# Planned waits of a recurrence in TensorE's order: five numbers of a table and one new entry

## The chip, the cores and the metric

The kernel runs on one core of one Trainium2 chip. The metric is the device time of one execution in microseconds; lower is better. Three executions took 3245.59 to 3251.01 us, with a median of 3248.01 us. PE, DVE, ACT, POOL and SP are TensorE, VectorE, ScalarE, GpSimd and SyncE; PEld is TensorE's loading of weights.

## What is computed

One layer over 2048 tokens of width 1024, in float32. Its heart is a delta rule with one 64x64 state per head, beside a pooling mixer and two gates; an MLP with squared ReLU and a gated embedding follow.

```python
def rwkv7_step(S, inp):
    r, w, k, v, kk, a = inp
    sa = jnp.einsum('bhvk,bhk->bhv', S, -kk)
    S = (S * w[:, :, None, :]
         + sa[..., None] * (kk * a)[:, :, None, :]
         + v[..., None] * k[:, :, None, :])
    y = jnp.einsum('bhvk,bhk->bhv', S, r)
    return S, y
...
    for i in range(DEPTH):
        h = rmsnorm(x, g_mix[i])
        z = h @ w_in[i]
        z_rwkv = token_shift(z[..., :RWKV_COLS], mu_shift[i])
        z_pool = z[..., RWKV_COLS:RWKV_COLS + POOL_WIDTH]
        gates = jax.nn.sigmoid(z[..., RWKV_COLS + POOL_WIDTH:] + b_gates[i])
        y_a = rwkv7_mix(z_rwkv, ...) @ w_out_a[i]
        y_b = multiscale_pool_mix(z_pool, pool_w[i], pool_scale[i]) @ w_out_b[i]
        merged = gates[:, :, 0] * y_a + gates[:, :, 1] * y_b
        x = x + merged @ w_o[i]
        h = rmsnorm(x, g_mlp[i])
        x = x + jnp.square(jax.nn.relu(h @ w_ff1[i])) @ w_ff2[i]
        h = rmsnorm(x, g_ple[i])
        x = x + jax.nn.sigmoid(h @ w_ple_gate[i]) * (p[i] @ w_ple_proj[i])
    return rmsnorm(x, g_final)
```

## The kernel before

**Two kinds of work in the first part.** The tokens lie in four blocks of 512. *Dense work* is `stage_A` of blocks 0 to 3 (the projections with `w_in`, the pooling mixer, the gates and `w_out_b`), then `stage_B` of blocks 0 to 3 (`w_out_a`, the merge, `w_o`). Each float32 product is three fp32r matmuls of 128x512 into banks named `d`; `big` holds the block's normed input (in stage B the merged branches), `yx` other operands (in stage B the recurrence's output for the block), `wf` the weights. The *recurrence* goes in 32 steps of 64 tokens, all heads at once, in banks named `rp` and `rc`.

**A step of the recurrence.** Its preparation (`prep_a`, `prep`) ends on TensorE in products with `bdb`, products with `bdk`, transposes of `bdv` and transposes of `BK`. Out of the products with `bdb` comes a matrix whose 32x32 blocks `invert` inverts: they go through memory on SP's queue (`aD`, `At`), 16 pairs of operations on VectorE make the inverse (L872 and L875, tiles `Xtmp` and `Xt`), and SP's queue brings it back as `xd` (`xD`, L876 and L840). Then `chain` runs, five groups of small matmuls, each of which reads what another engine made of the one before:

- TL: products of the state `SV`; ScalarE copies them to `Tn` (L890).
- first product: `xd` times `Tn`; ScalarE copies it to `U` and `VU`.
- aof: `aof` times `U`; VectorE subtracts it from `Tn` (L914).
- second product: `xd` times the new `Tn`; VectorE and ScalarE copy it to `VU` (L921, L923).
- NB: the new state `SVn`, made by VectorE; then the outputs by RD and Ct.

`gnorm` normalises the outputs; its transposes of `ybd` are TensorE's last work of a step, after which ScalarE, POOL and SP bring the result to `yaD` in memory (L968). `load_ya` reads a block of it back into `yx` (L389 to L391).

**What sets the order.** TensorE's order is written by a planner while the kernel is built (`drive`): a clock advances with each matmul, by 0.107 us or more. At a `yield LAT[...]` a step's generator hands in how long its next group has to wait by this clock. A group whose time has come goes next, the recurrence first; otherwise a piece of dense work is taken, three matmuls as a rule. The numbers of `LAT` are planned waits and make nothing wait on the chip: there TensorE works its list in order, and each matmul waits for its operands. The other engines' and the DMA queue's orders come from a scheduler that places the rest around TensorE's order. `C0` stands between the products with `bdk` and the transposes of `bdv`, `hop` after TL, `hu` after the first product and after aof, `hv` after the second product, `hs` after the outputs. A recurrence starts `inv` (47.1) after its products with `bdb` at the earliest, and when the one before has ended; the products with `bdk` wait until the recurrence two steps back has ended; `pace` and `pace2` set the distance of the steps.

**The rest.** From about 1605 us on the last block of stage B, the MLP (seven products in place of eight) and the embedding follow.

Of the kernel before, what the change touches and what calls it, by code (L numbers as in the profile page):

```python
# [36 lines left out]
C0 = math.exp(-0.5)  # L37
# [2 lines left out]
FS, WR = 2, 4  # L40
WS, WS2, WS3, WSB = 384, 384, 512, 512

LAT = dict(p0=11.7, p0b=15.8, A=17.7, B0=2.1, B1=5.6, C0=2.0, C1=4.9, C=8.8,
           hop=3.1, hu=2.8, hv=5.3, hs=3.0, inv=47.1, gn=17.8, pace=34.4, pace2=31.5)
TC_KW = dict(schedule_with_timeline_sim=True)

W1 = NP * UT
# [51 lines left out]
def hybrid_kernel(ctx, tc, consts, x, p, g_mix, w_in, mu_shift, w0, w_decay_up, a0, w_aaa_up,  # L99
# [28 lines left out]
    def mm(out_, lhsT, rhs, start, stop, **kw):  # L128
        n = 1
        for d in rhs.shape[1:]:  # L130
            n *= d
        clock[0] += max(0.107, n * (4 if rhs.dtype == F32 else 1) / 2370.0)
        PE.matmul(out_, lhsT, rhs, start=start, stop=stop, **kw)  # L133
# [62 lines left out]
    hs = chs.enter_context(tc.tile_pool(name="hs", bufs=1, side="left"))  # L196
# [4 lines left out]
    with ExitStack() as c1:  # L201
# [438 lines left out]
        def rps():  # L640
            return psum.tile([P, 512], F32, name="rp", tag="rp", bufs=2)

        def cps():
            return psum.tile([P, 512], F32, name="rc", tag="rc", bufs=2)

        aD = [dram.tile([4 * PC, SUB, SUB], F32, name=f"aD{i}") for i in range(2)]
        xD = [dram.tile([4 * PC, SUB, SUB], F32, name=f"xD{i}") for i in range(2)]
        HOP = LAT["hop"]

        def v3(t, w=UT):  # L650
            return t.rearrange("p (n t) -> p n t", t=w)

        def pq(t):

            return t.rearrange("p (q t) -> p q t", t=L)

        def wt(name, bufs=1, w=W1):
            return rw.tile([P, w], F32, name=name, bufs=bufs)
# [3 lines left out]
        def other(hp):  # L662
            return hps[1] if hp.start == 0 else hps[0]
# [77 lines left out]
        def prep(i):  # L741
# [34 lines left out]
            for hp in hps:  # L776
                ACT.copy(out=bdv[hp, :, other(hp)], in_=v_[hp])
            passed[0], passed[1] = i, max(clock[0] + LAT["B0"], began[0] + LAT["pace" if i < NU * 3 // 4 else "pace2"])
            yield LAT["B1"]

# [7 lines left out]
            for h in range(2):  # L788
                for d in range(2):
# [3 lines left out]
                                 in_=Ast[rows, :, d * SUB:(d + 1) * SUB])  # L793
            chain_ready[i] = clock[0] + LAT["inv"]
            yield None
# [8 lines left out]
            for hp in hps:  # L804
                DVE.tensor_tensor(by_pair(TL[hp, :, other(hp)]), by_pair(pv[hp, :, 0:L]), mbc(m_k, hp), ALU.mult)
                DVE.tensor_tensor(RD[hp, :, other(hp)], pv[hp, :, L:P], minc[hp].broadcast_to([L, PC, L]), ALU.mult)
            yield LAT["C0"]
            ps = rps()
# [8 lines left out]
            for h in range(2):  # L817
                for b in range(2):
                    lo, to = h * L + b * SUB, (1 - b) * SUB
                    POOL.tensor_copy(aof[lo:lo + SUB, :, h * L + to:h * L + to + SUB],  # L820
                                     Ast[lo:lo + SUB, b::2, to:to + SUB])
            yield LAT["C1"]
            NB = rw.tile([P, PC, P], F32, name="NB", bufs=2)
# [54 lines left out]
        def chain(i):  # L878

            c_ = carried[i]  # L880
            dl, xd, aof, Ct, NB, TL, RD, SV, VU = (c_[n] for n in ("dl", "xd", "aof", "Ct", "NB", "TL", "RD", "SV", "VU"))
            SVn = bd["SV"][(i + 1) % 2]
            Y = rw.tile([P, PC, L], F32, name="Y", bufs=2)
            c_["Y"] = Y
            qs = [(q, slice(q * L, (q + 1) * L), slice(q * P, (q + 1) * P)) for q in range(PC)]

            def diag(out_, ps):

                for hp in hps:
                    ACT.copy(out=out_(hp), in_=v3(ps, P)[hp, :, hp])  # L890
            ps = cps()
            for q, sl, wl in qs:
                mm(ps[:, wl], TL[:, q, :], SV[:, q, :], True, True)
            Tn = wt("Tn")
            diag(lambda hp: pq(Tn)[hp], ps)
            yield HOP
            q2s = [slice(a * P, (a + 1) * P) for a in range(PC // 2)]

            def quarters(src, inv):

                for n, (lo, b) in enumerate((h * L + b * SUB, b) for h in range(2) for b in range(2)):
                    yield n, VU[lo:lo + SUB, b ^ inv::2, lo // L * L:(lo // L + 1) * L], pq(src)[lo:lo + SUB, b ^ inv::2, :]
            ps = cps()
            for a, sl in enumerate(q2s):
                mm(ps[:, sl], xd[:, 2 * a, :], Tn[:, sl], True, True)
            Ua = wt("U")
            ACT.copy(out=Ua, in_=ps[:, 0:W1])
            for _, to, fr in quarters(ps[:, 0:W1], 0):
                ACT.copy(out=to, in_=fr)
            yield LAT["hu"]  # L910
            ps = cps()
            for a, sl in enumerate(q2s):
                mm(ps[:, sl], aof[:, a, :], Ua[:, sl], True, True)
            DVE.tensor_tensor(Tn, Tn, ps[:, 0:W1], ALU.subtract)  # L914
            yield LAT["hu"]
            ps = cps()
            for a, sl in enumerate(q2s):
                mm(ps[:, sl], xd[:, 2 * a + 1, :], Tn[:, sl], True, True)
            for n, to, fr in quarters(ps[:, 0:W1], 1):
                if n % 2:  # L920
                    DVE.tensor_copy(to, fr)  # L921
                else:
                    ACT.copy(out=to, in_=fr)  # L923
            yield LAT["hv"]
            ps = cps()
            for q, sl, wl in qs:
                mm(ps[:, wl], NB[:, q, :], VU[:, q, :], True, True)
            for hp in hps:
                DVE.tensor_tensor(SVn[hp, :, hp], v3(ps, P)[hp, :, hp], SV[hp, :, hp], ALU.add)
            for hp in hps:  # L930
                DVE.tensor_tensor(SVn[hp, :, hp], SVn[hp, :, hp], dl[hp].unsqueeze(2).broadcast_to([L, PC, L]), ALU.mult)
            py = cps()
            for q, sl, wl in qs:
                mm(py[:, wl], RD[:, q, :], SV[:, q, :], True, False)
                mm(py[:, wl], Ct[:, q, :], VU[:, q, :], False, True)
            diag(lambda hp: Y[hp], py)
            yield LAT["hs"]
# [43 lines left out]
        p0 = {}  # L981
# [4 lines left out]
        def admit():  # L986
            kinds = [k for k, *_ in active]
            i = counts["p0"]
            if i < NU and i == counts["a"] and i not in p0 and z_done[i // NG * UT // TB]:
                with tc.high_priority():  # L990
                    p0[i] = prep0(i)
                p0_ready[i] = clock[0] + (LAT["p0b"] if i % (NG * TB // UT) == 0 else LAT["p0"])
                counts["p0"] += 1
            i = counts["a"]
            if i in p0 and passed[0] >= i - 1 and max(p0_ready[i], passed[1]) <= clock[0]:
                with tc.high_priority():
                    pa[i] = prep_a(i)
                began[0] = clock[0]
                pa_ready[i] = clock[0] + LAT["A"]
                counts["a"] += 1  # L1000
            i = counts["prep"]
            if "prep" not in kinds and i in pa and i < counts["gn_done"] + 3:
                active.append(["prep", i, prep(i), pa_ready[i], None])
                counts["prep"] += 1
            i = counts["chain"]
            if "chain" not in kinds and i < counts["prep_done"] and i < counts["gn_done"] + 2:
                active.append(["chain", i, chain(i), chain_ready[i], None])
                counts["chain"] += 1
# [640 lines left out]
```

## Time and profile before

| | |
|---|---|
| median of three executions | 3248.01 us |
| profiled execution, its own time | 3247.18 us |
| its span, first to last instruction | 3245.4 us |
| TensorE busy | 3042.8 us (94%), mean granted clock 0.974 |
| VectorE busy | 2482.3 us (76%) |
| ScalarE, GpSimd busy | 1391.9 us (43%), 1228.0 us (38%) |

Rows of the profile name a line of the code (L133 and L137 are the helpers through which all matmuls and transposes go), the engine, the operation, and out<-in by the names of the tiles; buffer numbers are left out there and kept in the order below. A number in brackets, or behind the bar after the mean, is idle time of the engine just before, with what ended it. A group's time counts overlapping instructions once.

### The profile page before, as it was taken

The page shows a single profiled execution, that of the slowest core. Times are in us where ns is not written, and L with a number is a line of the kernel's source. Part 1 is how long each engine was busy: PE and PEld are TensorE (multiplying, and loading weights), DVE is VectorE, ACT ScalarE, POOL GpSimd, SP SyncE. Part 2 cuts the span into 40 slices and gives each one's busy share as a digit, 9 for nine tenths or more (in the row PEclk, how much of TensorE's full clock was granted, in tenths as well). Part 3 has the DMA queues.
Part 4 walks back from the last instruction along what each step waited for, and adds up shares of the span by engine and source line. Part 5 has one row for each costly group of instructions (what it writes and reads, how often), then busy time and mean ns, then how long its engine had stood idle before and what let it go on. Part 6 is the DMA issues. An engine that isn't in the chain of part 4 may idle for free. (4 is left out here: it accounts for less than half of the span.)

```text
span 3245.4 us, 43606 instructions
## 1 busy us (share of the span) xinstructions
PE 3042.8 (94%) x14409; PEld 2485.6 (77%) x14409; DVE 2482.3 (76%) x5419; ACT 1391.9 (43%) x2697; POOL 1228.0 (38%) x1325
## 2 busy tenths in 40 slices
PE   7999999899999998879989999999989999998998
PEld 6777777778777876758768788788768888886787
DVE  4479888788878888985478787866568898888665
ACT  4446654455445544533144444433243334333332
POOL 4555454345333534531125456555422232222100
PEclk9999999999999999989999999999989999999999
DMA  7776767666666666767865556544554465435331
GB/s 238 246 224 211 238 205 239 231 213 206 217 212 203 206 194 221 254 218 254 281 227 165 180 193 225 193 154 153 189 188 155 143 208 207 143 129 187 119 108 69
DMA packets 422702, 636.37 MB, mean 196 GB/s; under 512 B 173710, under 2 KB 285900, under 8 KB 391244
## 3 DMA queue, kind: packets, MB, share of 16 engines
q1 hardware_dynamic: 422476, 633.58, 59.1%
q8 instruction: 114, 1.87, 0.2%
q14 instruction: 112, 0.92, 0.1%
HBM read 439.49 MB, written 193.99 MB: 195 GB/s over the span
## 5 line engine op out<-in xcount | busy, mean ns | idle before, releaser
L133 PE MATMUL d<-big,wf 128*128 128x512 f32 (+1 forms) x3288 | 851.1, 407 | 21.2 <-DVE wf L244 8.0
L133 PEld LDWEIGHTS d<-big,wf 128*128 128x128 f32 x3288 | 609.8, 193 | 159.8 <-DVE wf L244 10.5
L133 PE MATMUL d<-op 128*128 128x512 f32 x1344 | 318.4, 396 | 19.1 <-ACT op L1111 15.0
L1112 POOL TENSOR_TENSOR op<-hr,op 128x1024 fp32r<-128x1024 f32 x56 | 153.1, 2734 | 459.4 <-ACT op L1111 459.4
L133 PEld LDWEIGHTS d<-op 128*128 128x128 f32 x1344 | 254.3, 189 | 78.2 <-ACT op L1111 15.4
L1111 ACT CAST op<-hr 128x1024 fp32r<-128x1024 f32 x112 | 117.7, 1051 | 355.9 <-issue 149.6
L1112 DVE TENSOR_TENSOR op<-w,op 128x1024 fp32r<-128x1024 f32 x112 | 181.3, 1620 | 108.0 <-ACT op L1111 108.0
L872 DVE TENSOR_TENSOR Xtmp<-Xt,At 128x16 f32<-128x16 f32 (+15 forms) x512 | 241.3, 471 | 9.3
L1112 POOL TENSOR_TENSOR op<-wr,op 128x512 fp32r<-128x512 f32 x96 | 144.7, 1508 | 244.7 <-ACT op L1111 241.5
L133 PE MATMUL d<-wf,big 128*128 128x512 f32 x768 | 200.8, 415 | 20.0 <-DVE t2k L611 17.8
L133 PE MATMUL d<-yx,wf 128*128 128x512 f32 x768 | 204.3, 412 | 15.9 <-ACT yx L390 7.3
L1293 POOL TENSOR_TENSOR t<-t,t 128x512 f32<-128x512 f32 x128 | 192.7, 1515 | 68.9 <-DVE t L1303 27.5
L133 PE MATMUL d<-wg,op 128*128 128x512 f32 x768 | 184.9, 396 | 12.8 <-ACT wg L1111 6.6
L133 PEld LDWEIGHTS d<-wf,big 128*128 128x128 f32 x768 | 146.8, 197 | 58.3 <-DVE t2k L611 22.1
L133 PEld LDWEIGHTS d<-yx,wf 128*128 128x128 f32 x768 | 145.7, 196 | 51.9 <-ACT yx L390 8.3
L1111 ACT CAST op<-wr 128x512 fp32r<-128x512 f32 x192 | 114.9, 619 | 156.9 <-DMA wr<-in_w_ff_dram 38.7
L133 PEld LDWEIGHTS d<-wg,op 128*128 128x128 f32 x768 | 146.2, 191 | 46.6 <-DVE wg L1112 7.3
L133 PE MATMUL rp<-op 128*128 128x512 f32 x672 | 171.3, 390 | 0.0
L133 PE MATMUL rc<-op 128*128 128x512 f32 x672 | 170.6, 389 | 0.0
L875 DVE TENSOR_REDUCE Xt<-Xtmp 128x8 f32<-128x16 f32 (+15 forms) x512 | 147.3, 288 | 9.2
L244 POOL TENSOR_TENSOR wf<-wr,wf 128x640 fp32r<-128x640 f32 (+2 forms) x69 | 121.7, 1764 | 78.7 <-ACT wf L241 74.4
L133 PEld LDWEIGHTS rp<-op 128*128 128x128 f32 x672 | 126.2, 188 | 26.9
(320 smaller groups left out, 6321.5 us busy)
## 6 DMA issues: line engine op xcount, KB each, us to landing
wf<-wc SPq DMA_DIRECT2D x131, 1024.0 KB, 5.1
wc<-wf SPq DMA_DIRECT2D x50, 1024.0 KB, 6.2
wr<-in_w_ff_dram SPq DMA_DIRECT2D x64, 512.0 KB, 3.8
w<-in_w_ff_dram SPq DMA_DIRECT2D x32, 1024.0 KB, 7.5
wr<-in_w_in_dram SPq DMA_DIRECT2D x51, 512.0 KB, 4.4
zD<-t2k SPq DMA_DIRECT2D x96, 256.0 KB, 4.0
zs<-zD SPq DMA_DIRECT2D x32, 640.0 KB, 6.2
At<-aD SPq DMA_DIRECT2D x32, 512.0 KB, 5.1
```

What stands on the lines that cost most here:

```text
L133: PE.matmul(out_, lhsT, rhs, start=start, stop=stop, **kw)
L244: eng.tensor_tensor(wf[:, 1, c], raw[:, c], hi.bitcast(F32)[:, c], ALU.subtract)
L872: DVE.tensor_tensor(tmp[:, :, :, 0:n], Xt[:, :, 0:n].unsqueeze(2).broadcast_to([P, MCOL, FS, n]), At[:, 0:n, r:n].rearrange("p s r -> p r ...
L875: DVE.tensor_reduce(Xt[:, :, r:n].unsqueeze(3), tmp[:, :, :, 0:n], AX.X, ALU.add)
L1111: ACT.copy(out=dst[0], in_=src)
L1112: eng.tensor_tensor(dst[1], src, dst[0].bitcast(F32), ALU.subtract)
L1293: eng.tensor_tensor(out_, a, b, op)
```

## The change

Five planned waits get other numbers, and the wait after aof gets an entry of its own, `ht`. Nothing else is edited.

```diff
-LAT = dict(p0=11.7, p0b=15.8, A=17.7, B0=2.1, B1=5.6, C0=2.0, C1=4.9, C=8.8,
-           hop=3.1, hu=2.8, hv=5.3, hs=3.0, inv=47.1, gn=17.8, pace=34.4, pace2=31.5)
+LAT = dict(p0=11.7, p0b=15.8, A=17.7, B0=2.1, B1=5.6, C0=4.6, C1=4.9, C=8.8,
+           hop=2.5, hu=2.6, ht=5.6, hv=6.2, hs=4.6, inv=47.1, gn=17.8, pace=34.4, pace2=31.5)
...
             for a, sl in enumerate(q2s):
                 mm(ps[:, sl], aof[:, a, :], Ua[:, sl], True, True)
             DVE.tensor_tensor(Tn, Tn, ps[:, 0:W1], ALU.subtract)
-            yield LAT["hu"]
+            yield LAT["ht"]
```

The same matmuls stand in another order. TensorE in the seventh step's recurrence, from TL to the second product (`plw` is the pooling mixer's weight, a product in full float32), before:

```order
L133 MATMUL rc<-SV_255,TL_251 128x128 x4
L133 MATMUL d<-big,wf 128x512 x12
L133 MATMUL d<-t2k,plw 128x512
L133 MATMUL rc<-Tn,xd_241 128x128 x2
L133 MATMUL d<-t2k,plw 128x512
L133 MATMUL d<-big,wf 128x512 x9
L133 MATMUL rc<-U,aof_247 128x128 x2
L137 MATMUL rp<-ident,ybd_245 128x128 x4
L133 MATMUL d<-big,wf 128x512 x12
L133 MATMUL rc<-Tn,xd_241 128x128 x2
```

The same place now:

```order
L133 MATMUL rc<-SV_255,TL_251 128x128 x4
L137 MATMUL rp<-ident,bdv_235 128x128 x4
L133 MATMUL d<-big,wf 128x512 x3
L133 MATMUL d<-t2k,plw 128x512 x2
L133 MATMUL rc<-Tn,xd_241 128x128 x2
L133 MATMUL d<-big,wf 128x512 x12
L137 MATMUL rp<-ident,BK 128x128 x4
L133 MATMUL rc<-U,aof_247 128x128 x2
L133 MATMUL d<-big,wf 128x512 x12
L133 MATMUL d<-yx,wf 128x512 x12
L133 MATMUL d<-big,wf 128x512 x3
L133 MATMUL rc<-Tn,xd_241 128x128 x2
```

Between aof and the second product stand 27 dense matmuls in place of 12, and before the first product fewer.

TensorE in the preparation of the eighth step, from `bdb` to the transposes of `bdv`, before:

```order
L133 MATMUL rp<-AR,bdb_231 128x128 x4
L133 MATMUL d<-big,wf 128x512 x3
L133 MATMUL rp<-AR,bdk_233 128x128 x4
L133 MATMUL d<-t2k,plw 128x512
L133 MATMUL d<-big,wf 128x512 x6
L137 MATMUL rp<-ident,bdv_235 128x128 x4
```

The same place now:

```order
L133 MATMUL rp<-AR,bdb_231 128x128 x4
L133 MATMUL d<-big,wf 128x512 x15
L133 MATMUL d<-t2k,plw 128x512
L133 MATMUL rp<-AR,bdk_233 128x128 x4
L133 MATMUL d<-big,wf 128x512 x6
L133 MATMUL rp<-sq,cst 8x64 x4
L133 MATMUL d<-big,wf 128x512 x15
L133 MATMUL rc<-SV_255,TL_251 128x128 x4
L137 MATMUL rp<-ident,bdv_235 128x128 x4
```

The products with `bdk` wait for a recurrence that ends later, and the transposes of `bdv` stand behind the start of the seventh step's recurrence.

TensorE at the end of the recurrence, from the last outputs to the first products of the last block's stage B (with `yx`), before:

```order
L133 MATMUL rc<-VU_260,Ct_239 128x128
L133 MATMUL d<-yx,wf 128x512 x6
L133 MATMUL d<-wf,big 128x512 x93
L137 MATMUL rp<-ident,ybd_245 128x128 x4
L133 MATMUL d<-wf,big 128x512 x99
L133 MATMUL d<-yx,wf 128x512 x96
```

The same place now:

```order
L133 MATMUL rc<-VU_260,Ct_239 128x128
L133 MATMUL d<-wf,big 128x512 x108
L137 MATMUL rp<-ident,ybd_245 128x128 x4
L133 MATMUL d<-wf,big 128x512 x42
L133 MATMUL d<-yx,wf 128x512 x96
```

The last transposes of `ybd` stand 42 matmuls ahead of the last block in place of 99.

## The prediction

> **What bounds the kernel now.** I read the clock and the stages first, then the waits of TensorE, then single waits in order of time. The first fence has the busy line of the page of the profile, the core's span, and three stretches (columns: microseconds, then busy time and instruction count of PE, PEld, DVE, ACT and POOL, granted clock, DMA share, GB/s).
>
> ```profile
> PE 3042.8 (94%) x14409; PEld 2485.6 (77%) x14409; DVE 2482.3 (76%) x5419; ACT 1391.9 (43%) x2697; POOL 1228.0 (38%) x1325
> core 0: 3245.4 us, clock 0.974
> 225.00:1270.00 1045.00, 984.65 (x5206) 812.34 (x5207) 886.64 (x2626) 543.52 (x1283) 446.58 (x716) 0.98 0.66 212
> 1270.00:1605.00 335.00, 287.98 (x1396) 233.68 (x1396) 240.13 (x618) 117.73 (x273) 116.98 (x135) 0.92 0.76 252
> 1605.00:3245.40 1640.40, 1570.83 (x6897) 1278.66 (x6896) 1233.64 (x1904) 623.42 (x957) 543.26 (x317) 0.98 0.49 168
> ```
>
> TensorE is the bound everywhere, so the time can fall by TensorE's idle time and by what its lower clock costs, and by nothing else. The change acts before 1605 us. There PE idles 1045 - 985 = 60 us in the steady stretch (stage A beside the recurrence) and 47 us in the next (stage B). What it waits for inside the recurrence: first the waits ahead of the two products with xd, then three groups whose second last figure is the idle time before them.
>
> ```profile
>   issue: 26.0, 9
>   DMA xd<-xD: 10.4, 1
>   ACT zp L512: 3.3, 2
>   ACT t2k L459: 1.9, 1
>   ACT wf L241: 1.5, 1
>   ACT ze L457: 1.2, 1
>   DVE Tn L914: 1.1, 1
>   ACT t2k L550: 0.9, 1
> L133 PE MATMUL rc<-VU,NB 128*128 128x128 f32 x256 | 35.1, 281 | 9.4 <-DVE VU L921 9.4
> L133 PE MATMUL rc<-U,aof 128*128 128x128 f32 x128 | 21.1, 290 | 4.8 <-ACT U L907 4.8
> L137 PE MATMUL rp<-ident,bdv 128*128 128x128 f32 x128 | 19.3, 273 | 1.4 <-DVE RD L806 1.4
> ```
>
> The eight rows sum to 46.3 us. The 10.4 us that a DMA ended stood before a first product; read in order of time, the other 35.9 us, 16 waits, all stand before the second. The longest shows why (start, duration, engine, and in brackets the idle time before):
>
> ```profile
> 480.97 0.67 PE L133 MATMUL rc<-U,aof 128*128 128x128 f32 x4
> 481.83 3.05 PE L133 MATMUL d<-big,wf 128*128 128x512 f32 x12
> 483.82 1.65 POOL L244 TENSOR_TENSOR wf<-wr,wf 128x640 fp32r<-128x640 f32 x1
> 484.42 1.34 DVE L872 TENSOR_TENSOR Xtmp<-Xt,At 128x160 f32<-128x160 f32 x1
> 489.06 0.50 DVE L872 TENSOR_TENSOR Xtmp<-Xt,At 128x208 f32<-128x208 f32 x1
> 489.48 0.41 DVE L914 TENSOR_TENSOR Tn<-Tn,rc 128x256 f32<-128x256 f32 x1
> 489.99 1.19 PE L133 MATMUL rc<-Tn,xd 128*128 128x128 f32 x4 [5.12 <-issue]
> L872 DVE TENSOR_TENSOR Xtmp<-Xt,At 128x160 f32<-128x160 f32 x32 | 17.7, 554 | 0.9
> ```
>
> The aof product was done at 481.6. Its subtraction (L914, 0.41 us) stood in VectorE's queue behind the next step's inverse (L872) and ended at 489.89; the second product began 0.1 us later. So the releasers named in the eight rows are not the cause; VectorE's place in its queue is. PE had 12 dense matmuls as cover and ran out.
>
> **The change part by part.** Dense matmuls give the rate, and four more of the 16 waits the sizes:
>
> ```profile
> 403.81 0.98 PE L133 MATMUL rc<-Tn,xd 128*128 128x128 f32 x3 [3.29 <-issue]
> 535.20 0.68 PE L133 MATMUL rc<-Tn,xd 128*128 128x128 f32 x4 [3.29 <-issue]
> 702.99 0.68 PE L133 MATMUL rc<-Tn,xd 128*128 128x128 f32 x4 [3.45 <-issue]
> 822.76 0.68 PE L133 MATMUL rc<-Tn,xd 128*128 128x128 f32 x4 [3.13 <-issue]
> 1578.22 23.26 PE L133 MATMUL d<-wf,big 128*128 128x512 f32 x99
> ```
>
> 23.26 / 99 = 0.235 us a matmul. *ht, 2.8 to 5.6.* The order puts some 27 dense matmuls where 15 or 12 stood, so 12 x 0.235 = 2.8 us more cover. Eleven of the 16 waits are shorter than that and go. The five longest keep 0.5 + 2.3 + 0.5 + 0.6 + 0.3 = 4.2 us. Gain 31.7 us, if L914 is as late as now; bounds 0 and 35.9.
>
> *hv, 5.3 to 6.2.* Three or four dense matmuls are added before NB in most steps, 0.8 us for each of the four waits that make up the 9.4 us: gain 3, bounds 0 and 9.4. *C0, 2.0 to 4.6*: the transposes of bdv waited 1.4 us, which goes. What is moved with it: the mask products of TL and RD on VectorE, the copies on ScalarE, the aof copies on POOL, and on SP the load of gg and the six reads of xd. These reads stand behind the inverse's own store, which is not moved, so I cost them at nothing; that cover is the first rival's subject.
>
> *hop, 3.1 to 2.5, and the first hu, 2.8 to 2.6.* Less cover: 12 dense and one plw product in the seventh step become 3, two plw and four transposes. What hides it is that ScalarE comes first:
>
> ```profile
> L890 ACT COPY Tn<-rc 64x256 f32<-64x256 f32 x64 | 23.4, 366 | 40.6 <-PE rc L133 40.1
> ```
>
> It idles 40.1 us in front of these copies, waiting for TensorE; the two take 0.7 us. Loss 1 us; bounds 0 and 32 x 3 matmuls x 0.235 = 23, if ScalarE were late each time.
>
> *Clock.* Half a dozen of the 16 waits are followed by a stretch at a lower clock. The first, the longest, one after a short wait with that wait's row, and the last:
>
> ```profile
> 400.00:410.00 10.00, 6.71 (x25) 5.29 (x24) 9.49 (x22) 2.76 (x7) 2.41 (x4) 0.83 0.73 213
> 486.00:498.00 12.00, 8.01 (x25) 6.45 (x25) 8.86 (x20) 1.20 (x3) 1.33 (x2) 0.72 0.74 214
> 1025.00:1034.00 9.00, 7.12 (x27) 5.38 (x25) 5.38 (x13) 3.44 (x8) 2.68 (x5) 0.81 0.58 186
> 1027.44 0.68 PE L133 MATMUL rc<-Tn,xd 128*128 128x128 f32 x4 [1.88 <-ACT t2k L459]
> 1145.00:1154.00 9.00, 6.70 (x25) 5.38 (x25) 6.70 (x15) 1.67 (x5) 2.04 (x3) 0.81 0.24 71
> ```
>
> A clock of 0.83 over 10 us is 1.7 us of work lost, 0.72 over 12 us 3.4; five times 1.7 and once 3.4 are 11.9 us. Since the longest wait stays in part, I take 9; bounds 0 and 11.9. The Trainium skill (TensorE: Matmul & The Clock Gate, Part 1) says that the clock falls after at least one idle window of about 3.4 us. By that rule only the waits of 5.12 and 3.45 us would cost clock, the term would be some 3 us, and the sum 6 us higher. The wait of 1.88 us with 0.81 behind it speaks against it, so the row decides.
>
> *Return of other waits.* VectorE gets the same 886.6 us of work in 1045 - 43 us: its idle share falls from 15.2% to 11.5%. The other 60 - 36 = 24 us of PE's idle time hang mostly on it and on ScalarE's queue. Scaled by 15.2 / 11.5 they grow by 8 us; bounds 0 and 24.
>
> *End of the part.* hs (3.0 to 4.6) delays nothing on PE by itself, since each recurrence starts by its inverse. But the planned waits of one recurrence sum to 21.5 where they summed to 17.0, so the last ends later, and the last transposes of ybd now stand 42 matmuls before the last block's first product with yx, not 99. What lies between:
>
> ```profile
> 1577.86 0.60 PE L137 MATMUL rp<-ident,ybd 128*128 128x128 f32 x4
> 1583.56 0.53 SPq L968 DMA_DIRECT2D yaD<-sq  x1
> 1585.95 1.76 SPq L389 DMA_DIRECT2D t2k<-yaD  x4
> 1591.09 0.69 DVE L391 TENSOR_TENSOR yx<-t2k,yx 128x512 fp32r<-128x512 f32 x1 [11.20 <-ACT yx L390]
> 1592.26 1.99 DVE L391 TENSOR_TENSOR yx<-t2k,yx 128x512 fp32r<-128x512 f32 x3 [0.48 <-ACT yx L390]
> ```
>
> From the transposes through the store and the loads on SP to the first block of yx are 13.9 us, to the last 16.4. 42 matmuls and the transposes cover 10.3. TensorE waits 4 us and loses 2 of clock: +6, bounds 3 and 14 (SP's queue held once more by a weight load ahead of the store).
>
> Sum: -31.7 - 3 - 1.4 + 1 - 9 + 8 + 6 = -30.1. The profiled execution took 3247.2 us around its span of 3245.4, so 3217.1; the median of the runs, 3248.0, is 0.8 above it: 3218.
>
> **The rivals.** *Slower: the inverse comes late.* The place is the first product with xd, which needs the 32x32 inverses that VectorE computes and SP carries. For it: the products with bdk move in the step shown from 3 to 16 matmuls behind those with bdb, so their masks fall into the inverse on VectorE; the one wait of 10.4 us lies in stage B, where the clock is 0.92. Against it: one such wait in 32 steps, and the start of a recurrence stays tied to bdb. The price is 10.4 + 3.4 of clock a time; more than 30 / 13.8 = 2.2 new ones spend the gain, and three give 3218 + 41 = 3259.
>
> *Same: the lag moves on.* VectorE keeps its list, and what PE does not wait for at the second product it waits for at NB or at a bank. For it: L872's 1.34 us against a mean of 0.554, beside a POOL instruction of 1.65 us; such meetings are drawn anew with the order. The Trainium skill (SBUF — State Buffer, Who interferes with whom) calls the port pair that VectorE and GpSimd share an exclusive lock; the row agrees, L872 ending 0.3 us after POOL's. Against it: NB also gets more cover. With gain (ht and clock) down to a quarter, 10 us, and 8 + 6 - 3.4 to pay, 3248.8; 3241 to 3254.
>
> *More:* L914 comes earlier in VectorE's list, no wait returns and the end costs 4: 3248 - 35.9 - 9.4 - 1.4 - 11.9 + 4 = 3193.
>
> That the change does nothing is excluded: the order shows the new distances.
>
> **How the numbers follow.** The likeliest, 3203 to 3232 around 3218, gets 0.55: the waits are counted, and the distances stand in the program. More gets 0.12, the moved lag 0.17, the late inverse 0.12, an end held by SP beyond its bounds 0.04. A measurement tells about 0.2%, 6.5 us. Faster by more: 0.55 + 0.12 and 0.03 of the moved lag, 0.70; same 0.13; slower 0.01 + 0.12 + 0.04 = 0.17. The range, 3196 to 3252, leaves out the two slow cases and a little at the bottom.
>
> **What would show it.** Right: the waits before xd other than by a DMA below 8 us, PE's idle time in the steady stretch near 35 us, fewer low-clock stretches, and a new wait for yx of 3 to 6 us at the first product of the last block. Wrong: waits before NB or before d that have grown by 20 us or more (the lag moved), or several waits for xd ended by its DMA (the inverse).

## The result, and the profile after

The changed kernel takes 3288.9 us (median of four, 3286.89 to 3295.13) where the kernel before, beside it, takes 3247.76: a ratio of 1.0129 [1.0115, 1.0143], 41 us slower. The forecast was 3218 us and 30 us faster. The profiled execution took 3295.13 us, the slowest of the four, so the two traces lie 48 us apart and not 41. First the busy line of the page of the changed kernel, and its core's span and clock.

```profile
PE 3056.4 (93%) x14409; PEld 2498.7 (76%) x14409; DVE 2484.3 (75%) x5419; ACT 1393.3 (42%) x2697; POOL 1206.6 (37%) x1325
core 0: 3293.3 us, clock 0.965
```

To compare like with like the first part is cut where the same work begins: at the first L611 of stage B, and at the last block's first product with `yx`. The L611 line (durations, first and last start) and that product, before:

```profile
L611 DVE SCALAR_TENSOR_TENSOR t2k<-t2k,d x32: 668/682/690, 1298.2 to 1634.7; 128x512 f32<-128x512 f32 x32
1601.31 16.96 PE L133 MATMUL d<-yx,wf 128*128 128x512 f32 x72
```

The L611 line of the changed kernel; its product with `yx` begins at 1647.06 and is shown further down:

```profile
L611 DVE SCALAR_TENSOR_TENSOR t2k<-t2k,d x32: 668/686/690, 1326.9 to 1682.4; 128x512 f32<-128x512 f32 x32
```

The stretches between these marks, columns as in the prediction, before:

```profile
190.00:1601.30 1411.30, 1301.48 (x6748) 1069.49 (x6747) 1151.07 (x3299) 679.44 (x1592) 582.27 (x874) 0.96 0.69 222
225.00:1298.20 1073.20, 1003.78 (x5306) 826.79 (x5307) 911.07 (x2690) 555.31 (x1306) 463.64 (x738) 0.97 0.67 214
1298.20:1601.30 303.10, 265.15 (x1280) 216.22 (x1280) 212.92 (x551) 105.94 (x249) 99.92 (x112) 0.93 0.74 247
```

And after:

```profile
190.00:1647.00 1457.00, 1310.61 (x6747) 1078.33 (x6745) 1150.15 (x3272) 680.83 (x1591) 557.45 (x873) 0.95 0.67 214
225.00:1326.90 1101.90, 1019.39 (x5339) 839.35 (x5337) 910.67 (x2659) 558.84 (x1310) 444.48 (x733) 0.96 0.65 208
1326.90:1647.00 320.10, 257.83 (x1244) 211.90 (x1244) 212.60 (x547) 105.33 (x247) 94.05 (x118) 0.89 0.70 234
```

The same 6748 matmuls take 45.7 us longer. TensorE is busy 9.1 us longer with them, at a lower clock, and idles 1457.0 - 1310.6 = 146.4 us where it idled 109.8. Some 29 us of the loss arise in stage A beside the recurrence, some 17 in stage B. From the last block on the rest takes 3293.3 - 1647.1 = 1646.2 us, against 1644.1 before: nothing more is lost there.

What ended TensorE's idle time in front of the products with xd, and the groups in the recurrence, after:

```profile
  ACT Tn L890: 7.8, 3
  issue: 5.8, 4
  ACT wf L241: 0.4, 1
L133 PE MATMUL rc<-VU,NB 128*128 128x128 f32 x256 | 36.0, 286 | 15.4 <-DVE VU L921 15.3
L133 PE MATMUL rp<-AR,bdb 128*128 128x128 f32 x248 | 34.8, 286 | 7.6 <-DVE bon L769 4.8 <-DVE bdb L766 2.7
L133 PE MATMUL rc<-U,aof 128*128 128x128 f32 x128 | 21.0, 289 | 10.6 <-ACT U L907 10.6
L137 PE MATMUL rp<-ident,bdv 128*128 128x128 f32 x124 | 19.2, 279 | 4.8 <-DVE RD L806 4.8
```

The waits that the change was aimed at are gone: 5.8 + 0.4 = 6.2 us stand before the second product, where 35.9 stood. Other places of the recurrence got worse: aof 4.8 to 10.6, NB 9.4 to 15.4, the products with bdb 0.5 to 7.6, the transposes of bdv 1.4 to 4.8. The first product, which had one wait of 10.4 us for xd, now has three for ScalarE's Tn, 7.8 us together. The largest growth is outside the recurrence, at the banks of dense work. Three of those waits before (from 190 us to the last block: total, times, longest):

```profile
PE d L133 <- DVE t2k L611: 17.1, 7, 4.0
...
PE d L133 <- DMA wf<-wc: 5.5, 3, 3.8
PE d L133 <- DVE t2k L636: 1.9, 4, 0.6
```

The same after, with one that is new:

```profile
PE d L133 <- DVE t2k L611: 28.9, 5, 11.3
...
PE d L133 <- DMA wf<-wc: 12.2, 6, 4.6
...
PE d L133 <- DVE t2k L636: 8.9, 2, 8.5
...
PE d L133 <- DVE rs_qg L154: 5.4, 1, 5.4
```

All such waits sum to 83.2 us, against 47.1, and a wait of 9.07 us at the end of the part, shown next, comes on top. So TensorE waits some 45 us more before d, and inside the recurrence some 9 us less: 146.4 - 83.2 - 9.1 = 54.1 us in place of 109.8 - 47.1 = 62.7. Last the end of the part, read in order of time, and the ten microseconds behind it:

```profile
1627.63 0.60 PE L137 MATMUL rp<-ident,ybd 128*128 128x128 f32 x4
1627.98 10.01 PE L133 MATMUL d<-wf,big 128*128 128x512 f32 x42
1633.23 0.53 SPq L968 DMA_DIRECT2D yaD<-sq  x1
1638.23 1.75 SPq L389 DMA_DIRECT2D t2k<-yaD  x4
1640.03 0.43 SPq L635 DMA_DIRECT2D t2k<-in_x_dram  x1
1643.64 1.33 DVE L391 TENSOR_TENSOR yx<-t2k,yx 128x512 fp32r<-128x512 f32 x2 [0.74 <-ACT yx L390]
1646.27 0.69 DVE L636 TENSOR_TENSOR t2k<-t2k,d 128x512 f32<-128x512 f32 x1 [1.29 <-DMA t2k<-in_x_dram]
1647.06 3.32 PE L133 MATMUL d<-yx,wf 128*128 128x512 f32 x7 [9.07 <-ACT junk L160]
1647.00:1657.00 10.00, 9.94 (x34) 7.97 (x35) 7.58 (x32) 0.34 (x2) 1.14 (x1) 0.76 0.88 309
```

The 42 dense matmuls run out at 1638.0, just as the loads of yaD are issued. TensorE waits 9.07 us, and a clock of 0.76 over the next ten (before it was 1.00 there) costs 2.4 more. The wait lasts beyond the last yx (1645.0). TensorE begins 0.1 us after L636 has read its bank d, so I take that bank to be what it waits for, and not the ScalarE instruction that the row names; the loads of x for L636 stood behind those of yaD on SP.

### The profile page after: what moved, and what is told of

The parts are those of the page before. It is cut to its first block, busy times and chain, and to the rows that moved or that the text cites. A ratio compares the mean times of both kernels' runs of the same rounds, so it can differ in the third digit from the quotient of the medians.

```text
span 3293.3 us, 43571 instructions
## 1 busy us (share of the span) xinstructions
PE 3056.4 (93%) x14409; PEld 2498.7 (76%) x14409; DVE 2484.3 (75%) x5419; ACT 1393.3 (42%) x2697; POOL 1206.6 (37%) x1325
## 5 line engine op out<-in xcount | busy, mean ns | idle before, releaser
L133 PEld LDWEIGHTS d<-op 128*128 128x128 f32 x1344 | 254.2, 189 | 78.5 <-ACT op L1111 15.4
L872 DVE TENSOR_TENSOR Xtmp<-Xt,At 128x16 f32<-128x16 f32 (+15 forms) x512 | 232.0, 453 | 10.4
```

The lines of the kernel that those rows point to most:

```text
L872: DVE.tensor_tensor(tmp[:, :, :, 0:n], Xt[:, :, 0:n].unsqueeze(2).broadcast_to([P, MCOL, FS, n]), At[:, 0:n, r:n].rearrange("p s r -> p r ...
```

## The experiments

Times are medians, with the ratio to the kernel before, run beside each, and its 95% interval. The median of the kernel before lay between 3247.8 and 3251.9 us beside them. Where an edit makes the table one line shorter, rows name lines one less.

### Which part of the change costs it

*ht alone* (before, with the new wait after aof):

```diff
-hop=3.1, hu=2.8, hv=5.3
+hop=3.1, hu=2.8, ht=5.6, hv=5.3
...
-            yield LAT["hu"]
+            yield LAT["ht"]
```

> Before, with ht 5.6 alone; the other five planned waits stay as before. Theory G (gate): a recurrence planned longer ends later, the products with bdk of the next preparation but one are held by it (planned hold 2.7 us a step in stage A, against 0.7 before and 5.1 in the changed kernel), and the masks fall into the inverse on VectorE; part of the loss: 3248 + 10 to 25 us, with the waits at the second product gone. Theory C (cover): the loss comes from hop and hu with too little cover; ht alone gains, 3210 to 3230. Theory R (rhythm drawn anew): every other order loses, whatever is changed; 3258 to 3290.

3269.52 us, 1.0068 [1.0049, 1.0086]. The group rows of the products with xd and of aof:

```profile
L132 PE MATMUL rc<-Tn,xd 128*128 128x128 f32 x256 | 41.5, 287 | 19.7 <-issue 8.3 <-ACT Tn L889 5.9 <-ACT t2k L490 1.7
L132 PE MATMUL rc<-U,aof 128*128 128x128 f32 x128 | 21.0, 289 | 12.1 <-ACT U L906 11.9
```

The waits with xd fall from 46.3 to 19.7 us, those before d rise from 47 to 70, and the kernel is 22 us slower: the term that carried the forecast costs time even by itself.

*All but ht* (the changed kernel with `ht=2.8`):

> The changed kernel with ht back at 2.8; C0, hop, hu, hv and hs as changed. G: planned hold 3.0 us a step, so 3248 + 10 to 25 us, the waits at the second product (35.9 us) being there as before. C: the short hop and hu lose here too: 3280 to 3310, with waits on Tn (L890) and U (L907) of 18 us or more. R: 3258 to 3290.

3264.18 us, 1.0042 [1.0025, 1.0059]. The other five numbers cost 14 us without ht. The two parts, 0.68% and 0.42%, come near the whole of 1.29%. Theory C is out by both runs; G and R both fit both.

*The new waits in steps 0 to 23 alone, and in steps 24 to 31 alone:*

```diff
+def planned(name, i):
+    return (NEW if i < 24 else OLD)[name]
...
-            yield LAT["hv"]
+            yield planned("hv", i)
```

> The six new waits in steps 0 to 23, beside stage A; the old ones in steps 24 to 31. If the parts add up: stage A loses the 29 us that it lost in the changed kernel, stage B and the end lose nothing: 3248 + 20 to 32 us. If the loss comes from the recurrence's late end: 3240 to 3252.

> The old waits in steps 0 to 23, the six new ones in steps 24 to 31. If the parts add up: stage A as before, stage B and the end lose the 8 and 13 us of the changed kernel: 3248 + 12 to 24 us, with a wait of some 9 us at the last block's first product with yx.

3274.34 us, 1.0075 [1.006, 1.009], and 3255.56 us, 1.0018 [1.0007, 1.0029]. Some 24 us come from the first 24 steps, as expected. The last eight cost 6, where 12 to 24 were expected, although the wait at the last block came (8.19 us). So the loss sits in no single place such as the end; the two parts sum to 30 of the 41 us.

### A new order by itself, and a recurrence that ends later

*Two numbers changed without a reason* (`B1` 5.6 to 6.0; `A` 17.7 to 18.1), to see what another order costs that is aimed at nothing:

> Before, with B1 (the wait from the end of prep's set-up to the products with bdb) 6.0 in place of 5.6: an edit that touches none of the recurrence's waits and adds 0.4 us where nothing waited. The hold of bdk stays at 0.7 us a step, but the order is drawn anew. Theory V (VectorE paces stage A: its list is worked in order, and what it idles at the head of the list is lost): the time moves with VectorE's idle time in stage A, up by 5 to 20 us, 3250 to 3270. Theory R (any other order loses, by whatever engine): 3258 to 3275. Theory G (the held bdk): no change, 3244 to 3252.

> Before, with A (the wait after prep_a) 18.1 in place of 17.7: a second edit without meaning for the recurrence. The same as for the last run: V 3250 to 3270 with VectorE's idle time, R 3258 to 3275, G 3244 to 3252.

3258.37 us, 1.0026 [1.0015, 1.0037], and 3257.89 us, 1.0022 [1.0012, 1.0032]. Each costs 7 us, so some 7 of the 41 us may need no mechanism of the change. Not every new order costs this: one that is redrawn late in the first part alone, shown last, gained 4 us.

*The recurrences started earlier again*, by what the change adds to their planned length: the changed kernel with `inv=42.6`, and ht alone with `inv=44.3`.

> The changed kernel, with inv 42.6 in place of 47.1: each recurrence may start 4.5 us earlier after its bdb, by as much as its planned waits have grown, so that it ends where it ended before; the planned hold of bdk is 1.3 us. xd had landed some 18 us before it was read. G: the loss goes, 3215 to 3250. C: hop and hu are as short as in the changed kernel, the time stays at 3280 to 3295. R: 3258 to 3290.

> Before, with ht 5.6 and inv 44.3 alone: the added planned wait of 2.8 us is taken off the start; planned hold of bdk 0.2 us a step, the distance between recurrences nearly even. G: the gain that I forecast for ht comes out, 3210 to 3235. C: the same, 3210 to 3230. R: 3258 to 3290.

3266.98 us, 1.0054 [1.004, 1.0069], and 3262.39 us, 1.004 [1.0027, 1.0053]. The first takes back some 24 of the 41 us, with all new waits kept inside the recurrence; the second some 9 of 22, with intervals that overlap. Theory G expected the whole loss to go in the first and a gain in the second, and neither came: with an end that is no later in the plan, ht still costs 13 us, a new order's price included.

*A late end and nothing else* (before, `hs` 3.0 to 7.5):

> Of the six numbers of the table, hs alone is changed, to 7.5. By the planner's clock each recurrence then ends 4.5 us later than before and the next preparation's products with bdk are held by 5.7 us a step, while no product inside the recurrence gets a shorter or longer planned wait; the distances of the steps stay regular. Theory 'late end' (what the change lost comes from recurrences that end later in the plan, which holds the preparation and brings the last transposes of ybd close to the last block): as many waits as in the changed kernel for the banks d and for NB, a wait for yx of 5 to 10 us, 3270 to 3290 us. Rival 'order inside the recurrence' (the loss comes from the uneven waits that ht, hop and hu make between its products): 3250 to 3260 us, which is before's time or a redraw above it.

3267.59 us, 1.0059 [1.0044, 1.0074]. The two groups that wait for the masks, and the last block's first product:

```profile
L136 PE MATMUL rp<-ident,bdv 128*128 128x128 f32 x124 | 20.4, 291 | 15.8 <-DVE RD L805 15.8
L132 PE MATMUL rp<-sq,cst 128*8 128x64 f32 x240 | 19.1, 224 | 13.8 <-DVE RD L805 13.8
1628.84 25.48 PE L132 MATMUL d<-yx,wf 128*128 128x512 f32 x96 [11.39 <-ACT yx L389]
```

A recurrence that ends 4.5 us later in the plan costs 17 us without one new distance inside it; what a new order costs by itself is in that figure. The wait for yx came, 11.39 us where 5 to 10 were expected. Before d 13 us were added (47 to 61), before NB none. Most others stand before the transposes of bdv and the products with sq: the products with bdk are held until the recurrence two steps back has ended, and VectorE's masks of them come late. In the changed kernel these waits are small (4.8 us); so a late end is shown to cost, but not by just these waits there.

### What a wait of TensorE is worth

*The second product freed of its wait.* L914 writes a tile that nobody reads, and the second product reads Tn as it was. TensorE's order stays the same.

```diff
-            DVE.tensor_tensor(Tn, Tn, ps[:, 0:W1], ALU.subtract)
+            Tm = rw.tile([P, W1], BF16, name="Tm", bufs=1)
+            DVE.tensor_tensor(Tm, Tn, ps[:, 0:W1], ALU.subtract)
```

> Before, with L914's difference written to a tile that nothing reads, so that the second product reads Tn as ScalarE left it and waits no longer for VectorE (the subtraction is left out of the result). TensorE's order is the one of before, VectorE has the same operations. Theory S (the waits are worth what they last, and the changed kernels lose by other things): the 16 waits of 35.9 us and their lower clock go, 3195 to 3212. Theory L (a wait taken away here comes back elsewhere in stage A, because what TensorE waits for is VectorE's and the weights' supply, not this product): stage A keeps more than half of it, 3225 to 3250, with more waits before NB and before d.

3245.69 us, 0.9987 [0.9978, 0.9997]. The groups with xd and NB:

```profile
L133 PE MATMUL rc<-Tn,xd 128*128 128x128 f32 x256 | 40.0, 280 | 9.8 <-DMA xd<-xD 9.8
L133 PE MATMUL rc<-VU,NB 128*128 128x128 f32 x256 | 40.0, 306 | 34.7 <-DVE VU L922 34.5
```

This is the run that settles the main term. All 35.9 us of waits before the second product are gone, by their cause and without a new order, and the time falls by 5 us. VectorE's queue is where it was, so TensorE meets it one group later: NB waits 34.7 us in place of 9.4. Up to the last block's first product, which began at 1597.4, TensorE's row is this:

```profile
190.00:1597.40 1407.40, 1295.76 (x6747) 1068.14 (x6747) 1151.12 (x3299) 677.43 (x1592) 580.76 (x873) 0.97 0.69 222
```

Its idle time there is 1407.4 - 1295.8 = 111.6 us, against 109.8 before. So the 35.9 us came back whole: 25.3 at NB, 4.2 at the transposes of bdv, 2.3 at aof, 1.2 at the products with sq and some 6 before d. The few us gained lie in TensorE's busy time, 1295.8 in place of 1301.5.

*ScalarE in VectorE's place, first for VU, then for L914 too:*

```diff
-                if n % 2:
-                    DVE.tensor_copy(to, fr)
-                else:
-                    ACT.copy(out=to, in_=fr)
+                ACT.copy(out=to, in_=fr)
```

> The kernel before, with VectorE's two copies of VU after the second product (L921) given to ScalarE, so that NB no longer waits for VectorE. Theory 'the lag is VectorE's and moves on': the waits before NB (9.4 us) go, but those before the second product (35.9 us, for L914) stay or grow: 3235 to 3255 us. Rival (each wait is worth its length): 9.4 us less and no more, 3238 to 3242 us, with the waits before the second product as they were.

3245.32 us, 0.9984 [0.9972, 0.9996]. NB waits no more, the products with xd wait as before (47.3 us); 5 us are gained for 9.4 us of waits. The time lies in the range of the first theory and 3 us above the rival's.

```diff
-                mm(ps[:, sl], aof[:, a, :], Ua[:, sl], True, True)
-            DVE.tensor_tensor(Tn, Tn, ps[:, 0:W1], ALU.subtract)
+                mm(ps[:, sl], aof[:, a, :], Ua[:, sl], True, False)
+                mm(ps[:, sl], nid, Tn[:, sl], False, True)
+            ACT.activation(out=Tn, in_=ps[:, 0:W1], func=AF.Copy, scale=-1.0)
```

> As the run before, and L914 goes too: Tn is subtracted on TensorE by a second matmul into the bank of aof (with minus the identity as weight), and ScalarE copies the bank to Tn with its sign turned. TL to NB then wait for no instruction of VectorE. Theory 'the lag moves on' says that this must take away the waits at both places, 35.9 and 9.4 us, since the next place where TensorE waits for VectorE is SVn a step later: TensorE idles 20 to 45 us less in stage A and the time is 3200 to 3235 us. Rival (VectorE's queue comes back at the banks d, which it also frees): waits before d grow by 20 us or more and the time is 3238 to 3255 us. Cost on TensorE by itself: 64 more small matmuls, some 10 us if nothing covers them, which is in both figures.

3265.24 us, 1.0063 [1.0042, 1.0084]. Its control has the same products in the same order, and VectorE as before:

```diff
+                mm(ps[:, sl], zid, Tn[:, sl], False, True)
             DVE.tensor_tensor(Tn, Tn, ps[:, 0:W1], ALU.subtract)
```

> The control for the run in which ScalarE does L914 and all of VU: TensorE has the same instructions in the same order as there, with a matrix of zeros in place of minus the identity, and VectorE does L914 and its two copies of VU as before. The two differ by the waits for VectorE inside the recurrence and by the 27 us of VectorE's work that go with them, and by nothing on TensorE. If the waits are worth their length, this kernel has some 40 us of waits before the second product and NB and stands 30 to 45 us above that one: 3295 to 3310 us. If the lag only moves on, it has these waits and 20 to 40 us less of others (before d and the products with bdb), and stands within 8 us of it: 3257 to 3273 us.

3276.27 us, 1.0076 [1.0048, 1.0104]. The control's longest wait before xd, its wait before NB, and two of its waits elsewhere (total, times, longest):

```profile
PE rc L133 <- issue: 32.5, 9, 5.0
...
PE d L133 <- ACT wf L241: 7.1, 3, 4.4
PE d L133 <- DMA wf<-wc: 5.5, 1, 5.5
...
PE rc L133 <- DVE VU L924: 4.3, 3, 1.8
```

The run without them:

```profile
PE d L133 <- DMA wf<-wc: 15.5, 6, 7.1
PE d L133 <- ACT wf L241: 13.2, 3, 6.2
...
PE rp L133 <- DVE bdb L768: 11.6, 6, 3.7
...
PE rc L133 <- ACT Tn L917: 1.0, 1, 1.0
```

Before xd and NB some 50 us of waits are gone. Waits for wf and bdb have taken much of their place: TensorE's idle time up to the last block falls only from 120.7 to 110.3 us. The pair differs by 11 us in the medians and by 0.13% (4 us) in the ratios, whose intervals overlap. The control stands 3 us above the range of the lag that moves on, and 19 below that of waits worth their length. A microsecond of wait taken away inside the recurrence gained 0.1 to 0.2 us by this pair, 0.1 by the freed second product, and 0.5 by the copies of VU. The gain expected of the first of the pair, 3200 to 3235 us, did not come, and its time lies above the rival's range as well.

### VectorE's work

*Half of the inverse left out, before and after:*

```diff
-            for r in range(0, SUB, FS):
+            for r in range(0, SUB // 2, FS):
```

> Before, with the second half of the inverse left out (8 of the 16 pairs L872 and L875 of every step, the longer ones), so VectorE has some 250 us less to do; the result is not the reference's. TensorE's planned order is unchanged. V: VectorE no longer lags, the waits before the second product fall from 35.9 us to under 10, and the time falls by 30 us or more, below 3218. R: it falls by the waits removed at most, 3215 to 3250.

> The changed kernel, with the same half of the inverse left out. V: without VectorE's lag the two orders are worth the same: within 10 us of the light kernel with the order of before. R: the changed order still costs 25 us or more against that one.

3185.63 us, 0.9798 [0.9783, 0.9812], and 3217.38 us, 0.9908 [0.9881, 0.9934]. The two lines of the inverse from 225 to 1605 us, before:

```profile
L872 DVE TENSOR_TENSOR Xtmp<-Xt,At 128x32 f32<-128x32 f32 (+1 forms) x495 | 232.3, 469 | 9.1
L875 DVE TENSOR_REDUCE Xt<-Xtmp 128x8 f32<-128x32 f32 (+1 forms) x495 | 142.6, 288 | 8.9
```

With half of it left out:

```profile
L872 DVE TENSOR_TENSOR Xtmp<-Xt,At 128x48 f32<-128x48 f32 (+1 forms) x246 | 84.4, 343 | 2.6
L875 DVE TENSOR_REDUCE Xt<-Xtmp 128x8 f32<-128x32 f32 (+1 forms) x247 | 53.9, 218 | 2.9
```

So VectorE matters much: 65 us. But with a light VectorE the change still costs 32 us by the medians (0.9908 against 0.9798), where it is 41 with a full one. TensorE's rows up to the last block, with the order of before and with the changed one:

```profile
190.00:1540.70 1350.70, 1285.81 (x6751) 1061.21 (x6750) 938.84 (x2788) 679.25 (x1592) 567.64 (x873) 0.98 0.72 232
190.00:1567.90 1377.90, 1282.36 (x6740) 1056.82 (x6739) 941.03 (x2763) 679.48 (x1591) 561.18 (x872) 0.97 0.71 227
```

TensorE's idle time grows from 64.9 to 95.5 us, while the waits before the second product are 3.7 and 1.8 us. So most of the loss does not need the lag at that product. A part does hang on VectorE's load: up to the first L611 the change costs 15 us here (1267.3 against 1252.0 us) and 29 with a full VectorE.

*Less work elsewhere on VectorE, TensorE's order as before* (the copies of VU on ScalarE, and these):

```diff
-            DVE.tensor_scalar(sa, sa, 0.5, 0.5, op0=ALU.mult, op1=ALU.add)
+            ACT.activation(out=sa, in_=sa, func=AF.Identity, scale=0.5, bias=hb[:, 0:1])
...
-        DVE.tensor_scalar(h, src, -0.5, None, op0=ALU.mult)
...
-            DVE.tensor_tensor(q, q, h, ALU.mult)
+            DVE.scalar_tensor_tensor(q, q, -0.5, src, op0=ALU.mult, op1=ALU.mult)
```

> TensorE's order as before. Some 47 us of VectorE's work in the first part go without any wait of TensorE being aimed at: the two copies of VU (L921, 18.6 us) and the half-angle step of the sigmoids (L701, 14.1 us) go to ScalarE, and the reciprocal root does without its product by minus one half (L151, 14.0 us), which is folded into another instruction with the same rounding. Theory 'VectorE's amount of work sets the time, not its place in front of a product': the inverse cut by half took some 187 us from VectorE and gave 65 us, 0.35 us for each us; here that gives 16 us, so 3228 to 3240 us, with the waits before the second product still there in part (15 to 36 us). Rival (only work ahead of L914 in the queue counts): 3240 to 3250 us.

3251.97 us, 1.0002 [0.999, 1.0014]: nothing, where 16 us were expected. VectorE's busy time from 225 to 1605 us fell from 1126.8 to 1097.3 us, by 29.5 and not by the 47 that were forecast. The halved inverse took 1151.1 - 938.8 = 212 us from VectorE and gave 65; at that rate 29.5 us are worth 9, and these did not come either. What ends VectorE's wait at the head of the inverse (L862), before:

```profile
L862 DVE TENSOR_TENSOR Apr<-At 128x512 f32<-128x512 f32 x30 | 37.5, 1251 | 47.3 <-DMA At<-aD 47.1
```

With less work, and TensorE's longest row before the products with xd:

```profile
L862 DVE TENSOR_TENSOR Apr<-At 128x512 f32<-128x512 f32 x30 | 40.7, 1358 | 58.6 <-DMA At<-aD 58.5
  issue: 30.0, 12
```

VectorE comes earlier to the inverse and waits there for `At`, which comes back from memory only after TensorE's products with bdb. L914 stands behind the inverse and comes about as late as before: TensorE waits 38.2 us before the second product. So less work on VectorE was not by itself a gain here. That ScalarE, which took part of it over, gave a gain back is not excluded. What the halved inverse shortened is the chain from bdb through memory and sixteen dependent pairs: 16 x (0.469 + 0.288) = 12.1 us a step became 8 x (0.343 + 0.218) = 4.5. That the chain's length is the price is my reading of the two runs together; it was not tried apart.

*The distance of the steps in stage B* (`pace2` 31.5 to 32.2), alone and on top of the run above:

> Before, with pace2 32.2 in place of 31.5: steps 24 to 31 are set a little further apart, and TensorE's order is drawn anew in stage B alone. In the other seven kernels stage B took 2 to 11 us less than before's 306 us, except in the changed one. If that stretch of before is a poor draw: 3236 to 3244; if not: 3246 to 3256.

> The run before with pace2 32.2 in place of 31.5, the redraw of stage B that gave 0.13% by itself. If both gains hold beside each other, 4 us under the run before, 3224 to 3236 us; if the 0.13% was luck of one order, the same as that run or up to 7 us more.

3245.37 us, 0.9987 [0.9976, 0.9999], and 3238.37 us, 0.9963 [0.9952, 0.9973]. The first lies between its two ranges, the second 2 us above its own. The second is the fastest full kernel of this study and beats both. Its last block begins at:

```profile
1588.66 14.24 PE L133 MATMUL d<-yx,wf 128*128 128x512 f32 x60 [1.18 <-DVE rs_qn L152]
```

That is 12.7 us earlier than before. It gains 14 us on the run with the same relief and the old pace, more than the 4 expected; why the two help each other is open.

## Why the prediction was wrong

**ht, gain 31.7 us: the step that failed.** Its count was right: 6.2 us of waits remain where 4.2 were forecast. So "if L914 is as late as now" is not what failed. What failed is the price: each wait went into the sum with its whole length, as if TensorE met VectorE's queue at no other place. With the cause of the 35.9 us taken away in the same order, TensorE idled as long as before (111.6 us against 109.8) and the time fell by 5 us; ht alone made the kernel slower by 22.

**Clock, gain 9.** It hung on the same waits and went the other way: the clock fell from 0.97 to 0.96 in stage A and from 0.93 to 0.89 in stage B, and TensorE was busy 9.1 us longer with the same matmuls. That the longer waits before d are the reason was not tried apart.

**hv, gain 3, and C0, gain 1.4.** NB waits 6.0 us more, bdv 3.4 more. Each lay beyond its bounds, on the side of a loss that these bounds, 0 at worst, did not allow.

**hop and hu, loss 1.** The first product waits 7.8 us for ScalarE's Tn and aof 5.8 us more for U: 13.6 us, within the bounds of 0 and 23. That ScalarE idled 40.1 us before these copies was an average over steps, and did not cover the three and four places where its copies came late.

**Return of other waits, loss 8.** The waits before d alone grew by 83.2 - 47.1 = 36 us, and by 9.07 more at the end. The prediction named a growth of 20 us there as the sign that it is wrong.

**End of the part, loss 6, bounds 3 and 14.** 9.07 + 2.4 = 11.5 us. The mechanism and the bounds held. The missing piece is the loads of x behind those of yaD, some 2 us of the wait.

**What no term held.** The planned end of each recurrence, later by 4.5 us, was costed at nothing but the end of the part. Alone it costs 17 us, and an earlier start takes back 24 of the 41. Each of these kernels has a new order too, and two orders that were drawn anew without a purpose cost 7 us each, so the 17 and the 7 may not be added. Some 17 to 24 us are left without a shown cause. The uneven waits inside the recurrence are the candidate: ht without the late end still costs 13 us.

**The rivals.** The moved lag was the right mechanism for the main term (0.17), at the places it named: NB in the kernel with the second product freed, the banks d in the changed kernel. Its 3248.8 us (by its own terms 3248.6) missed the loss, since it kept the small costs of the other terms. The late inverse did not come: no wait before xd is ended by its DMA any more.

The Trainium skill's rule on the clock (TensorE: Matmul & The Clock Gate, Part 1) would have made the clock's term 3 us by the prediction's estimate; no run here puts the two sizes apart, since the waits did not go but moved.

## What to carry to other kernels

A wait in a trace tells where two in-order engines meet, not what it costs. Before its length goes into a sum, take the wait's cause away in a kernel with the same order, and see where the next one opens. Where an order comes from a planner, redraw it once or twice by a meaningless number, so that the price of a new order is known, and ask of every planned delay what the plan starts only after its end.

## What the runs showed of the hardware

The same order does not take the same time to the microsecond in its parts: with TensorE's order unchanged up to there, the same transposes of bdv began at 1165.7 us in the kernel before and at 1169.4 in the one with the new pace2, whose order differs only behind them. A few us of difference in one trace's stage are therefore no finding, and the verdicts above go by medians.

An engine with less to do did not make the program faster: VectorE was busy 29.5 us less and the time stayed the same, while VectorE's wait for one DMA grew from 47.1 to 58.5 us.
